# First norm of a hybrid decoder step: shift and scale in 256, 256 and 512 features, and a new order around them

## The chip, the cores and the metric

The kernel runs on one core of a Trainium2 chip. A core has a matrix engine (TensorE, PE), a vector engine (VectorE, DVE), a scalar engine (ScalarE, ACT), a general engine (GpSimd, POOL) and a queue engine that issues transfers (SyncE, SP); 16 DMA engines move data between HBM and the on-chip memory. The metric is device time in microseconds (us), the median of several runs. The kernel before takes 1035.17 us (three runs, 1034.39 to 1036.36).

## What is computed

One layer of a decoder trunk for 512 prompt tokens and 8 sample tokens (520 columns), model width 1024. What matters here is its beginning:

```python
def rms_norm(x, g):
    xf = x.astype(jnp.float32)
    y = xf * lax.rsqrt(jnp.mean(xf * xf, axis=-1, keepdims=True) + EPS)
    return (y * g.astype(jnp.float32)).astype(x.dtype)

def ada_modulation(c, ada_w, ada_b):
    m = (jax.nn.silu(c) @ ada_w + ada_b)[:, None, :]
    return jnp.split(m, 6, axis=-1)
...
    sh1, sc1, g1, sh2, sc2, g2 = ada_modulation(c, ada_w, ada_b)
    h = rms_norm(x, norm1_g) * (1.0 + sc1) + sh1
    z = h @ w_in
    cuts = list(np.cumsum([D_RNN, D_RNN, ATTN_W, ATTN_W, ATTN_W, N_HEADS, D_MODEL]))
    xr, gr, q, k, v, fl, ga, gb = jnp.split(z, cuts, axis=-1)
```

Behind it come a gated recurrence, attention over the prompt and over paged caches, the merge of both branches and a gated feed-forward part. All of it is float32, and each product of two float32 matrices is made of three products of parts.

## The kernel before

**Layout.** Activations stand transposed: a tile has 128 features on the partitions and 520 tokens as columns, so the width of 1024 is eight tiles, called features 0 to 7 below. Columns are worked on in two halves of 260 (`HALVES`); the last 8 columns are the sample tokens. Every operand of a product is split in a high part (a cast to the matmul type, `hi`, on ScalarE) and a low part (the rest, `lo`, on VectorE); one product is three matmuls, hi x hi, lo x hi and hi x lo (L527).

**The start, in program order.**
1. SP loads the parameters, the constants, the eight tiles of `x`, and the page table twice (`ptb`, `idx`, L424 and L426).
2. ScalarE squares `x` (L536), VectorE adds up (L538), TensorE sums over the partitions (`ss`, L543).
3. `first_mod` (L470) computes shift and scale of the first norm for half of the features, 512 at a time: for each of eight k it loads a block of `ada_w` (`araw`, 512 KB) and issues four matmuls, one for each group of 32 columns of the array (L476), 256 columns wide. `first_mod_end` (L480) copies the sum (`adas`), transposes it twice (`adaft`), adds the bias to get `mod` (L489) and forms the amplitude `n1amp` (L493).
4. The square root (L548) and the reciprocal (L549) give the reciprocal norm `r1`, and eight multiplications give `xn` (L552).
5. `first_h` (L496) makes the operand of a feature: ScalarE's `hh` (L499) for 512 prompt columns, GpSimd's two small operations for the 8 sample columns (L500, L501), ScalarE's cast of these (L503), VectorE's copy of the modulated tile (L502) and the low part `hl` (L504).
6. `q_weights` (L507) loads and splits the weights of two column tiles of q for four features: `wraw`, `whi` (L517), `wlo` (L518).
7. The products for the first six tiles of q run in two halves of the features. The first half (features 0 to 3) runs over two groups of three tiles, `g3` = 0 and 3, each with six PSUM banks, in an order k, tile, half of the columns. In the first group a k of the second `first_mod` (features 4 to 7) is placed behind every third product; in the second group, behind k = 0, stands its `first_mod_end` and `first_h` for features 4 to 7. The partial sums are copied out (L575). Then the weights of the second half are loaded and split, and a scheduler of products (`begin`, `product`) takes over, which adds the second half's sums (`qp`, L902).

**What sets the order.** The tile framework puts each engine's instructions in an order of its own from the program and its estimate of times; `tc.issue_after` holds instructions back behind a named one. Engines work through their own list in order. Buffers come from pools: seven for `araw` and cache pages (`pgp`), two for `wraw`, three each for `whi` and `wlo`, eight PSUM banks. An instruction that writes a buffer waits for the last reader of what was in it. GpSimd's gather of past forget values (`past_load`, L431) uses a `wraw` buffer. SP's transfers share eight semaphores, so each waits for the landing of the eighth before it.

Of the kernel before, what the change touches and what calls it, by code (L numbers as in the profile page):

```python
# [8 lines left out]
F32 = mybir.dt.float32  # L9
# [9 lines left out]
NP = 512  # L19
NS = 8  # L20
NT = NP + NS
H = 16
# [42 lines left out]
def kernel(ctx, tc, xT, par, gates, b_f, cst, cse, own, cache_k, cache_v, cache_lf, pt,  # L65
# [358 lines left out]
    sp.dma_start(ptb, pt.rearrange("a b -> (a b)")[None, :])  # L424
    idx = keep.tile([NS * NPAGE, 1], I32, name="idx")
    sp.dma_start(idx, pt.rearrange("a (b c) -> (a b) c", c=1))  # L426
# [43 lines left out]
    def first_mod(fh, acc, kqs):  # L470
        for kq in kqs:
            raw = pgp.tile([128, 2, 512], F32, name="araw", tag="pg")
            sp.dma_start(raw, ada_w[kq * 128:kq * 128 + 128, :2048].rearrange("p (v c) -> p v c", v=2)
                         [:, :, 512 * fh:512 * fh + 512])
# [5 lines left out]
    def first_mod_end(fh, acc):  # L480
        sb = slot("adas", 256)
        act.copy(sb, acc[:, :256])
        tp = bank(f"adaft{fh}")
        for b in range(2):
            pe.transpose(tp[:, b * 128:b * 128 + 128], sb[:, b * 128:b * 128 + 128], ident)
        tv = tp[:, :256].rearrange("p (b g c) -> p b g c", b=2, g=4)
        fs = slice(4 * fh, 4 * fh + 4)
        for v in (1, 0):
            dve.tensor_tensor(  # L489
                mod[:, v, fs].rearrange("p (q b) c -> p b q c", b=2), tv[:, :, 2 * v:2 * v + 2, 0:9],  # L490
                prm[:, fs, P_AB + v:P_AB + v + 1].rearrange("p (q b) c -> p b q c", b=2).to_broadcast([128, 2, 2, 9]),
                ALU.add)
        dve.scalar_tensor_tensor(amp1[:, fs], mod[:, 1, fs], 1.0, prm[:, fs, P_N1:P_N1 + 1].to_broadcast([128, 4, 9]),  # L493
                                 ALU.add, ALU.mult)
# [13 lines left out]

    def q_weights(fh, raw, ko, i):
# [5 lines left out]
        for k in range(0, 4, 2 if (fh, i) == (0, 0) else 4):  # L515
            ks = slice(k, k + 2 if (fh, i) == (0, 0) else 4)
            state["act"] = act.copy(hi[:, ks], src[:, ks])  # L517
            state["last"] = dve.tensor_tensor(lo[:, ks], src[:, ks], hi[:, ks].bitcast(F32), ALU.subtract)  # L518
# [25 lines left out]
    acc = [bank(f"adaf{fh}") for fh in range(2)]  # L544
    first_mod(0, acc[0], range(KT))
    r1 = slot("r1")
    for j, (t0, t1) in enumerate(HALVES):
        act.activation(r1[:, t0:t1], ssq[j][:, :HALF], AF.Sqrt, bias=eps, scale=1.0 / D)  # L548
        dve.reciprocal(r1[:, t0:t1], r1[:, t0:t1])  # L549
    for f in range(KT):  # L550
        t = slot("xn")
        dve.tensor_tensor(t, x[f], r1, ALU.mult)  # L552
        xn.append(t)
    raw = wraw()
    q_weights(0, raw, 0, 0)
    first_mod_end(0, acc[0])
    for f in range(4):
        first_h(f)
    q_weights(0, raw, 4, 2)
    raw = wraw()  # L560
    q_weights(0, raw, 0, 4)
    for g3 in (0, 3):
        banks = [bank(f"qp{i}_{j}") for i in range(g3, g3 + 3) for j in range(2)]
        for k in range(4):
            for n in range(6):
                q_matmuls(0, g3 + n // 2, n % 2, k, banks[n])
                if g3 == 0 and n % 3 == 2:
                    first_mod(1, acc[1], (2 * k + n // 3,))
            if g3 and k == 0:
                first_mod_end(1, acc[1])  # L570
                for f in range(4, KT):
                    first_h(f)
        for n in range(6):
            t0, t1 = HALVES[n % 2]
            act.copy(qpart[g3 + n // 2][:, t0:t1], banks[n][:, :HALF])  # L575
        if g3 == 0:
            flr = slot("flr", KT * H).rearrange("p (k c) -> p k c", k=KT)
# [1148 lines left out]
```

## Time and profile before

| | |
|---|---|
| median of three runs | 1035.17 us (1034.39 to 1036.36) |
| the profiled execution | 1036.26 us, span 1034.6 us |
| TensorE busy in 0 to 10, 10 to 20, 20 to 30 us | 0.38, 8.70, 7.11 us |
| TensorE busy in 30 to 60 us | 30.0 of 30 us |
| TensorE busy in 200 to 1034.6 us | 809.7 of 834.6 us |
| first product of q | 25.18 us after the span's start |
| first product of the second half of the features | 50.70 us |
| DMA moved | 207 MB, mean 200 GB/s |

Each profile is of one execution; times in it count from the span's start. Busy time of TensorE includes the tail of each matmul, which overlaps the next one, so what one matmul costs is read from the distance between starts. "Idle before, releaser" in brackets names the wait of that engine ahead of the row and what ended it.

### The profile page before, as it was taken

The page shows a single profiled execution, that of the slowest core. Times are in us where ns is not written, and L with a number is a line of the kernel's source. Part 1 is how long each engine was busy: PE and PEld are TensorE (multiplying, and loading weights), DVE is VectorE, ACT ScalarE, POOL GpSimd, SP SyncE. Part 2 cuts the span into 40 slices and gives each one's busy share as a digit, 9 for nine tenths or more (in the row PEclk, how much of TensorE's full clock was granted, in tenths as well). Part 3 has the DMA queues.
Part 4 walks back from the last instruction along what each step waited for, and adds up shares of the span by engine and source line. Part 5 has one row for each costly group of instructions (what it writes and reads, how often), then busy time and mean ns, then how long its engine had stood idle before and what let it go on. Part 6 is the DMA issues. An engine that isn't in the chain of part 4 may idle for free.

```text
span 1034.6 us, 21301 instructions
## 1 busy us (share of the span) xinstructions
PE 993.8 (96%) x7994; PEld 920.1 (89%) x7994; DVE 795.3 (77%) x1416; ACT 549.4 (53%) x1128; POOL 333.9 (32%) x431
## 2 busy tenths in 40 slices
PE   4999999999999999999999999999999999999994
PEld 2888989999898988878888989999999999999993
DVE  5547999988989977886665555878888888888763
ACT  4523675856682267776794234554444444445451
POOL 0224511112133235544430001494343342444022
PEclk9999999999999999999999999999999999999997
DMA  9898987787888999988675783324334234133222
GB/s 332 294 295 290 301 286 213 259 250 275 257 238 309 324 310 300 300 252 269 202 267 198 254 286 104 82 63 123 90 95 123 74 112 123 42 103 103 64 70 74
DMA packets 165419, 206.99 MB, mean 200 GB/s; under 512 B 9906, under 2 KB 126146, under 8 KB 165250
## 3 DMA queue, kind: packets, MB, share of 16 engines
q1 hardware_dynamic: 148594, 152.52, 47.7%
q0 software_dynamic: 13040, 46.67, 13.7%
q10 hardware_dynamic: 3680, 6.42, 1.7%
q8 instruction: 63, 1.03, 0.4%
q14 instruction: 42, 0.34, 0.1%
HBM read 192.49 MB, written 13.09 MB: 199 GB/s over the span
## 4 chain that ended last, share of the span: by engine, by line
PE 70%; DVE 12%; DMA 6%; ACT 4%; issue 4%; POOL 2%; SPq 1%; POOLq 0%; ACTq 0%; DVEq 0%
PE fo L305 9%; PE pb L305 4%; PE gb L305 4%; PE xr L305 3%; PE ga L305 3%; PE k L305 3%; PE wo L305 3%; PE v L305 3%; DVE wlo L250 2%; PE gr L305 2%; PE qp L527 2%; DVE pg L730 2%; PE pv L815 2%; PE po L1258 2%; PE ada L368 1%
## 5 line engine op out<-in xcount | busy, mean ns | idle before, releaser
L248 ACT CAST whi<-wraw 128x1024 fp32r<-128x1024 f32 (+1 forms) x79 | 82.0, 1039 | 117.9 <-PE pb L305 35.0
L250 DVE TENSOR_TENSOR wlo<-wraw,whi 128x1024 fp32r<-128x1024 f32 (+1 forms) x79 | 101.3, 1284 | 30.1 <-ACT whi L248 25.9
L305 PE MATMUL fo<-ach,wb 128*128 128x260 f32 x512 | 93.3, 282 | 0.0
L272 ACT CAST wb<-ws 128x512 fp32r<-128x512 f32 x72 | 44.8, 622 | 91.2 <-PE fo L305 63.6
L682 POOL DMA_DIRECT2D pg<-in_cache_k_dram x74 | 39.6, 535 | 142.4 <-DVE S L731 70.3
L305 PEld LDWEIGHTS fo<-ach,wb 128*128 128x128 f32 x512 | 78.8, 188 | 0.0
L273 DVE TENSOR_TENSOR wb<-ws,wb 128x512 fp32r<-128x512 f32 x72 | 67.5, 937 | 14.6 <-ACT wb L272 12.6
L273 DVE TENSOR_TENSOR wb<-wraw,wb 128x512 fp32r<-128x512 f32 x86 | 74.2, 863 | 5.1 <-ACT wb L272 4.4
L263 POOL TENSOR_TENSOR ws<-wraw 128x512 f32<-128x512 f32 x18 | 26.6, 1478 | 154.0 <-DMA wraw<-in_w_fi_dram 76.7
L305 PE MATMUL fo<-acl,wb 128*128 128x260 f32 x256 | 72.3, 282 | 0.0
L272 ACT CAST wb<-wraw 128x512 fp32r<-128x512 f32 x86 | 53.6, 623 | 33.6 <-ACT cp L1612 5.8
L730 DVE TENSOR_TENSOR pg<-pg,qb 128x1024 f32<-128x1024 f32 x48 | 58.0, 1227 | 2.5 <-DMA pg<-in_cache_k_dram 2.5
L731 DVE TENSOR_REDUCE S<-pg 128x16 f32<-128x1024 f32 x48 | 57.0, 1207 | 0.1
L1215 POOL TENSOR_SCALAR p<-p,mu 128x128 f32<-128x128 f32 (+3 forms) x28 | 35.9, 1294 | 49.9 <-DVE mu L1211 33.1
L397 POOL TENSOR_TENSOR ss<-ss,sq 128x260 f32<-128x260 f32 x18 | 13.8, 769 | 110.3 <-PE ada L368 58.9
L305 PEld LDWEIGHTS fo<-acl,wb 128*128 128x128 f32 x256 | 48.1, 188 | 0.0
L1209 ACT ACTIVATE p<-p,mu 128x128 f32<-128x128 f32 (+3 forms) x64 | 35.3, 553 | 15.9 <-DVE mu L1208 12.4
L305 PE MATMUL v<-hh,whi 128*128 128x260 f32 x128 | 37.3, 291 | 1.3 <-DVE pl L1229 1.3
L305 PE MATMUL ga<-hh,wlo 128*128 128x260 f32 x128 | 36.9, 288 | 0.9 <-DVE wlo L250 0.9
L305 PE MATMUL pb<-oh,whi 128*128 128x260 f32 x128 | 36.7, 287 | 1.0 <-ACT oh L1316 1.0
L305 PE MATMUL k<-hh,whi 128*128 128x260 f32 x128 | 37.3, 291 | 0.0
L305 PE MATMUL ga<-hh,whi 128*128 128x260 f32 x128 | 37.0, 289 | 0.0
(1092 smaller groups left out, 3990.7 us busy)
## 6 DMA issues: line engine op xcount, KB each, us to landing
araw<-in_ada_w_dram SPq DMA_DIRECT2D x48, 512.0 KB, 6.8
wraw<-in_w_fi_dram SPq DMA_DIRECT2D x44, 512.0 KB, 4.7
pg<-in_cache_k_dram POOLq DMA_DIRECT2D x42, 512.0 KB, 5.5
pg<-in_cache_v_dram SPq DMA_DIRECT2D x42, 512.0 KB, 5.8
wraw<-in_w_in_dram SPq DMA_DIRECT2D x34, 512.0 KB, 8.1
wraw<-in_w_in_dram SPq DMA_DIRECT2D x11, 1024.0 KB, 9.8
pg<-in_cache_v_dram POOLq DMA_DIRECT2D x22, 512.0 KB, 6.3
pg<-in_cache_k_dram POOLq DMA_DIRECT2D x32, 256.0 KB, 6.0
```

The lines of the kernel that those rows point to most:

```text
L248: state["act"] = act.copy(hi[:, :k1 - k0], src)
L250: state["last"] = dve.tensor_tensor(lo[:, :k1 - k0], src, hi[:, :k1 - k0].bitcast(F32), ALU.subtract)
L263: pool.tensor_tensor(s1, a21, a22, ALU.add)
L272: state["act"] = act.copy(t[:, :4], src)
L273: state["last"] = dve.tensor_tensor(t[:, 4:], src, t[:, :4].bitcast(F32), ALU.subtract)
L305: state["mm"] = pe.matmul(out[:, :HALF], lhsT=wt[k], rhs=at, start=k == 0 and m == 0, stop=k == nk - 1 and m == 2)
L527: state["mm"] = pe.matmul(b[:, :HALF], lhsT=wt, rhs=at[:, t0:t1], start=k == 0 and m == 0, stop=k == 3 and m == 2)
L682: done.append(eng.dma_start(pg, cache[bass.ds(r, 1), :, c0:c1].rearrange("a p c -> (a p) c")))
L730: dve.tensor_tensor(pg, pg, q, ALU.mult)
L731: last = dve.tensor_reduce(S[r // 2][:, c:c + H], pg.rearrange("p (h d) -> p h d", d=DH), AX.X, ALU.add)
L1209: act.activation(p[:, :n + 128], p[:, :n + 128], AF.Exp, bias=mu[:, 0:1], scale=-1.0, accum_out=mu[:, 1:2])
L1215: (pool.tensor_scalar(p, p, mu[:, 2:3], None, ALU.mult) if a and i + 1 < KT else act.activation(p, p, AF.Copy, scale=mu[:, 2:3]))
```

## The change

The modulation of the first norm comes in three parts instead of two: features 0 and 1 (256 columns), features 2 and 3 (256), features 4 to 7 (512). For the first two parts, blocks of 256 KB (`qraw`, rows of 1 KB) are loaded two to a buffer, and each matmul has 128 columns (`quarter_load`, `quarter_mod`). The first part stands ahead of the products, the second among the products of features 0 and 1, the third among those of features 2 and 3 of the first group and of features 0 and 1 of the second.

The reciprocals stand first on VectorE. For features 0 and 1, `xn`, `hh` and `hl` are made by halves of the columns (`early_norm`, `early_h`), and `xn` is modulated in place; the other `xn` follow. The weights of the first half of q are loaded for three column tiles and two features at a time (`q_load`, 384 KB) and split in `q_high` and `q_low`. The products of the first half go in groups (`q_group`) in an order half of the columns, feature, tile, not feature, tile, half. The loads of `ptb` and `idx` move behind these loads.

Cut to its core; `q_weights` and the copies are only rearranged:

```diff
-    sp.dma_start(ptb, pt.rearrange("a b -> (a b)")[None, :])
     idx = keep.tile([NS * NPAGE, 1], I32, name="idx")
-    sp.dma_start(idx, pt.rearrange("a (b c) -> (a b) c", c=1))
...
+    def quarter_load(q, kq):
+        if kq % 2 == 0:
+            quarters[q, kq // 2] = pgp.tile([128, 2, 2, 256], F32, name="qraw", tag="pg")
+        sp.dma_start(quarters[q, kq // 2][:, kq % 2],
+                     ada_w[kq * 128:kq * 128 + 128, :2048].rearrange("p (v c) -> p v c", v=2)
+                     [:, :, 256 * q:256 * q + 256])
+
+    def quarter_mod(q, acc, kqs):
+        for kq in kqs:
+            raw = quarters[q, kq // 2][:, kq % 2]
+            for g in range(4):
+                pe.matmul(acc[32 * g:32 * g + 32, :128], lhsT=silc[:, kq],
+                          rhs=raw[:, g // 2, 128 * (g % 2):128 * (g % 2) + 128],
+                          start=kq == 0, stop=kq == KT - 1, tile_position=(0, 32 * g))
...
+    def early_norm(j):
+        t0, t1 = HALVES[j]
+        for f in range(2):
+            state["last"] = dve.tensor_tensor(xn[f][:, t0:t1], x[f][:, t0:t1], r1[:, t0:t1], ALU.mult)
+
+    def early_h(j):
+        t0, t1 = HALVES[j]
+        e_ = min(t1, NP)
+        for f in range(2):
+            if j == 0:
+                h.append((slot("hh", dt=F32R), slot("hl", dt=F32R)))
+            t, (hi, lo) = xn[f], h[f]
+            a_, b_ = amp1[:, f, 0:1], mod[:, 0, f, 0:1]
+            first = act.activation(hi[:, t0:e_], t[:, t0:e_], AF.Identity, scale=a_, bias=b_)
+            if j:
+                pool.tensor_tensor(t[:, NP:], t[:, NP:], amp1[:, f, 1:9], ALU.mult)
+                pool.tensor_tensor(t[:, NP:], t[:, NP:], mod[:, 0, f, 1:9], ALU.add)
+                act.copy(hi[:, NP:], t[:, NP:])
+            dve.tensor_scalar(t[:, t0:e_], t[:, t0:e_], a_, b_, ALU.mult, ALU.add)
+            dve.tensor_tensor(lo[:, t0:t1], t[:, t0:t1], hi[:, t0:t1].bitcast(F32), ALU.subtract)
+        return first
...
-    first_mod(0, acc[0], range(KT))
+    raw = wp.tile([128, 4, 384], F32, name="wraw", tag="wraw", bufs=2)
+    for kq in range(6):
+        quarter_load(0, kq)
+    q_load(raw, 0, 0)
+    for kq in range(6, KT):
+        quarter_load(0, kq)
+    quarter_mod(0, accs[0], range(KT))
+    for kq in range(KT):
+        quarter_load(1, kq)
...
-        dve.reciprocal(r1[:, t0:t1], r1[:, t0:t1])
-    for f in range(KT):
-        t = slot("xn")
-        dve.tensor_tensor(t, x[f], r1, ALU.mult)
-        xn.append(t)
-    raw = wraw()
-    q_weights(0, raw, 0, 0)
-    first_mod_end(0, acc[0])
-    for f in range(4):
+        state["last"] = dve.reciprocal(r1[:, t0:t1], r1[:, t0:t1])
+    early_norm(0)
+    his = q_high(raw, 0, 0, 1)
+    with tc.issue_after(state["last"].ins):
+        q_low(*his, 0)
+    with tc.issue_after(first_mod_end(0, 1, accs[0]).ins):
+        first = early_h(0)
+        q_low(*his, 1)
+        early_norm(1)
+        with tc.issue_after(first.ins):
+            early_h(1)
+    for f in range(2, KT):
+        dve.tensor_tensor(xn[f], x[f], r1, ALU.mult)
+    q_load(raw, 2, 0)
+    q_split(raw, 2, 0)
+    sp.dma_start(ptb, pt.rearrange("a b -> (a b)")[None, :])
+    sp.dma_start(idx, pt.rearrange("a (b c) -> (a b) c", c=1))
...
+    q_group(0, 0, 0)
+    q_group(0, 0, 1, (0, 1), quarter)
+    q_group(0, 1, 0, (2, 3, 4), quarter)
+    q_group(0, 1, 1, (5, 6, 7), quarter)
+    first_mod_end(2, 1, accs[1])
+    first_h(2)
+    first_h(3)
+    acc = bank("adaf2")
+    q_group(0, 0, 2, (0,), half)
...
+    q_group(0, 1, 2, (1,), half)
+    q_group(0, 0, 3, (2,), half)
+    q_group(0, 1, 3, (3, 4), half)
...
+    q_group(3, 0, 0, (5,), half)
+    q_group(3, 1, 0, (6,), half)
+    q_group(3, 0, 1, (7,), half)
+    first_mod_end(4, 2, acc)
...
+    for f in range(4, KT):
         first_h(f)
...
+    for j, k in ((1, 1), (0, 2), (1, 2), (0, 3), (1, 3)):
+        q_group(3, j, k)
```

In `q_group(i0, j, k, kqs, mod)` the products of three tiles from `i0` with feature `k` are issued for half `j` of the columns, and then the modulation of the given `kqs`.

104 lines of the change are left out of this document (64 added, 40 removed).

## The prediction

> **What bounds the kernel now.** I read the page's busy shares first, then the start in stretches of ten microseconds (columns: busy time and count of TensorE, its weight loads, VectorE, ScalarE and GpSimd, then TensorE's clock, DMA share, GB/s).
>
> ```profile
> span 1034.6 us, 21301 instructions
> PE 993.8 (96%) x7994; PEld 920.1 (89%) x7994; DVE 795.3 (77%) x1416; ACT 549.4 (53%) x1128; POOL 333.9 (32%) x431
> ```
>
> ```profile
> 0.00:10.00 10.00, 0.38 (x1) 0.38 (x2) 2.10 (x3) 5.29 (x8) 0.56 (x7) 1.00 0.78 264
> 10.00:20.00 10.00, 8.70 (x56) 3.86 (x55) 7.83 (x9) 3.57 (x6) 0.00 (x0) 1.00 1.04 385
> 20.00:30.00 10.00, 7.11 (x45) 4.69 (x46) 8.71 (x17) 6.74 (x13) 4.81 (x8) 0.66 1.07 370
> ```
>
> TensorE idles 40.8 us in all, 13.8 of them in the first 30 us (9.6 + 1.3 + 2.9); in the other 1004.6 us it idles 27. So TensorE sets the time, and a change at the start is worth what it does to the moment at which TensorE has finished the same work. The chain of waits (start, duration, step) says what holds it there.
>
> ```profile
> 16.04 7.11 DMA wraw<-in_w_in_dram
> 23.15 0.02 issue
> 23.18 1.14 ACT whi L517 x2
> 24.31 0.82 ACT hh L499
> ...
> 25.18 3.85 PE qp L527 x15
> ...
> 33.39 1.28 PE qp L527 x9
> 34.67 0.57 PE adaf L476 x8
> ...
> 44.36 6.50 PE qp L527 x54
> ```
>
> The reader is to see three things. The first q product waits until 25.18 for transfers and then for a cast and the first `hh`. From there TensorE works without a gap. A q matmul takes 6.50 / 54 = 0.120 us. One k of the modulation (four matmuls over 256 columns, eight records) takes 0.57, and a round of nine products and one such k takes 1.85, so each switch between the two kinds costs 1.85 - 0.57 - 9 x 0.120 = 0.20 more. The first half of q (features 0 to 511) ends at 44.36 + 6.50 = 50.9. That moment is my yardstick: what does the change make of it, and of the products right behind it?
>
> **Part 1, the first product comes earlier.** Before it, VectorE now does two reciprocals, two half-width `xn`, one low part of 384 columns and the three small operations on `mod`, in place of two reciprocals, eight full `xn` and those three. Its rows (start, duration, operation), and ScalarE's:
>
> ```profile
> 14.24 3.42 DVE L549 RECIPROCAL r<-r 128x260 f32<-128x260 f32 x2 [1.84 <-ACT r L548]
> 17.69 4.97 DVE L552 TENSOR_TENSOR xn<-x,r 128x520 f32<-128x520 f32 x8
> ...
> 23.85 0.30 DVE L489 TENSOR_TENSOR mod<-adaft,prm 128x36 f32<-128x36 f32 x2 [1.19 <-PE adaft L485]
> 24.08 0.20 DVE L493 SCALAR_TENSOR_TENSOR n1amp<-mod,prm 128x36 f32<-128x36 f32 x1
> ...
> 50.56 0.70 DVE L504 TENSOR_TENSOR hl<-hr,hh 128x520 fp32r<-128x520 f32 x1
> 51.18 1.22 DVE L518 TENSOR_TENSOR wlo<-wraw,whi 128x1024 fp32r<-128x1024 f32 x1
> 52.34 0.43 DVE L902 TENSOR_TENSOR qp<-q,qp 128x260 f32<-128x260 f32 x1
> ```
>
> ```profile
> 14.60 0.48 ACT L548 ACTIVATE r<-ss,eps 128x260 f32<-128x260 f32 x1 [0.39 <-PE ss L543]
> ...
> 42.95 1.05 ACT L517 CAST whi<-wraw 128x1024 fp32r<-128x1024 f32 x1
> ...
> 46.51 0.20 ACT L503 CAST hh<-hr 128x8 fp32r<-128x8 f32 x1 [0.83 <-POOL hr L501]
> 46.61 0.82 ACT L499 ACTIVATE hh<-xn,mod,n1amp 128x512 fp32r<-128x512 f32 x1
> ```
>
> The reciprocals end at 17.66 in both kernels, because nothing ahead of them changes. Two `xn` of 260 columns (0.43 alone, about 0.35 back to back) reach 18.4; the low part of 384 columns, between 0.43 and 0.70, reaches 18.9; `mod` twice and `n1amp` (24.28 - 23.85 = 0.43) reach 19.3; the half-width `hh` (0.48, as the square root of that width) 19.8. First product at 19.9.
>
> The other branch is the transfers (TensorE's rows):
>
> ```profile
> 21.70 0.95 PE L476 MATMUL adaf<-araw,silc 128*32 128x256 f32 x8 [0.73 <-DMA araw<-in_ada_w_dram]
> 23.13 0.69 PE L485 MATMUL adaft<-cs,adas 128*128 128x128 f32 x2 [0.47 <-ACT adas L482]
> ```
>
> Now 8 x 512 KB = 4.19 MB have landed at 21.70. The changed kernel needs 8 x 256 KB and one weight block of 384 KB, 2.49 MB, so 1.70 MB less. At the 383 GB/s of the stretches below that is 4.4 us: 17.3. Its rows are 1 KB instead of 2 KB; where 1 KB weight rows land the stretch shows 351 GB/s, which adds 0.65: 17.9. Modulation, copy and transpose, half as wide, take about 1.1 where 21.70 to 23.85 is 2.15 now: `mod` could begin at 19.0. Both branches meet, and I keep 19.9, a gain of 5.3; bounds 19.7 and 21.0. The eight or so added transfer issues on SP, and the two page-table loads moved behind them, are covered: issues run ahead of landings, and the gather that needs the page table starts at 54.72 (row in part 4). GpSimd's register reads of that table now stand between the small additions for features 1 and 2, which part 3 puts some 5 us apart.
>
> **Part 2, work that comes back behind the start.** Before, half of the modulation lay in front of the first product; now only a quarter does, and the second quarter stands among the products. That is eight k of 128 columns. No row has that width. A k of 512 columns takes
>
> ```profile
> 85.48 0.99 PE ada L368 x8
> ```
>
> so 0.57 at 256 and 0.99 at 512 give 0.36 at 128 on a straight line; the upper bound is 0.57, if the eight weight loads and not the columns set it. I take 0.36: 2.9 in all. They stand in four places, four switches of 0.20; one more transpose is 0.1. Sum +3.8; bounds 3.0 and 5.5. VectorE's and ScalarE's halved instructions for features 0 and 1 (six more on VectorE) lie beside these products; if that cover failed they would cost about half a microsecond.
>
> **Part 3, a wait for features 2 and 3.** The first 36 products use features 0 and 1 alone. What follows the last k of the second quarter is: copy, transpose, `mod` twice, `n1amp`, together about 1.2, then `hh` of 512 columns 0.8, 2.0 in all. TensorE has, meanwhile, the transpose, one modulation k and one product, 0.8. So it idles +1.2; bounds 0 (other engines ahead) and 2.0.
>
> **Part 4, a wait at the second half.** In the order in which the changed program is built, ScalarE's third weight cast for the second half stands ahead of `hh` of features 6 and 7, and it needs the buffer that the very last product of the first half reads. GpSimd's gather of the past forget values, which needs that cast's low part, now stands ahead of the last small addition for feature 7; in the kernel before, it stands behind all of them:
>
> ```profile
> 48.23 0.57 POOL L501 TENSOR_TENSOR hr<-hr,mod 128x8 f32<-128x8 f32 x1
> 54.72 1.21 POOL L431 DMA_INDIRECT lfp<-in_cache_lf_dram,idx  x1 [5.93 <-DVE wlo L518]
> ```
>
> Count from the end E of the last product of the first half. Cast 1.05: E+1.1. `hh` of feature 6 0.82: E+1.9, and TensorE, which has 12 products of features 4 and 5 (1.45), waits 0.4. Low part 1.22 and `hl` 0.70: E+3.0, TensorE waits 0.6. Gather, 0.3 behind the low part as now: E+2.6 to E+3.9; addition 0.4 to 0.6, copy 0.2: E+4.6; TensorE, at E+3.5 by then, waits 1.1. Behind that copy stand the six copies that free the PSUM banks: 0.2 more. Sum +2.3; bounds 0 and 3.0.
>
> **Part 5, the clock.** Stretches of TensorE (busy time, clock, DMA share, GB/s):
>
> ```profile
> 18.53:21.94 3.41, 1.78 (x28) 0.99 1.06 372
> 21.94:25.35 3.41, 1.58 (x11) 0.50 1.09 351
> 25.35:28.76 3.41, 3.41 (x15) 0.51 1.05 386
> 11.70:15.10 3.40, 2.66 (x13) 1.00 1.03 383
> ```
>
> Now the products from 25.18 to 28.76 run at half clock, a loss of 1.8. The clock fell behind a stretch that was 52% busy and did not behind one that was 78% busy. In the changed kernel the stretch 18.53 to 21.94 would be about 60% busy (from 19.9 on). That is nearer to 52%, but where such a stretch lies in another execution no row says, so I count half of the loss as saved, -0.9; bounds 0 and -1.8. [...]
>
> **The sum.** -5.3 + 3.8 + 1.2 + 2.3 - 0.9 = +1.1 us. The profiled execution took 1036.26 (span 1034.6 and 1.66 around it), 1.1 above the median 1035.17 of the runs (1034.39 to 1036.36). From the first hundred microseconds on, both programs issue the same instructions in the same order, and TensorE has next to no slack there, so I let the shift stand and put it on the median: 1036.3.
>
> **Rivals.**
> - A, slower. The 128-column k cost 0.57 like the 256-column ones, at the same eight weight loads. Place: the second quarter among the first 36 products. Price 8 x 0.21 = 1.7, time 1038.0. For it: eight records start 0.07 us apart whatever waits. Against: 256 to 512 columns cost 0.42 more. It decides from 0.49 us for one k, where the sum passes +2.1.
> - B, faster. The waits of parts 3 and 4 do not show, because casts, gather and copies come before TensorE needs them: 1036.3 - 3.5 = 1032.8. For it: the kernel before has the same kinds of hand-over at 44 us without a gap. Against: the buffer and queue order just told.
> - C, the clock stays full through the start, for a reason that the 52% row does not cover: 1035.4. For it: work resumes 5 us earlier. Against: that row. [...]
> - D, the change does not do what it says: the 1 KB rows hold the first quarter back to the bound of 21.0, so the first product comes 4.2 earlier, not 5.3: 1037.4. Against: both branches reach 19.9 independently.
>
> **How the numbers follow.** About 0.2% (2.1 us) can be told from no change. The forecast, no measurable change at 1036.3, has 0.34; its own range is 1034.5 to 1038.0. A has 0.23, B 0.26, C 0.12, D 0.05. Faster is B, 0.26. Slower is A with 0.03 of D and the upper edge of the forecast, 0.03: 0.29. The rest, 0.45, is no change. All favourable bounds (-5.5 + 3.0 - 1.8) give 1030.9, all unfavourable (-4.2 + 5.5 + 2.0 + 3.0) 1041.5; a tenth of the chance left out on each side gives 1032.2 to 1039.2.
>
> **What would show each step.** Part 1: first `qp` matmul near 19.9, VectorE busy from the reciprocals to `n1amp`. Part 2: eight records of the small modulation in about 0.36 (0.57 speaks for A). Part 3: about 1.2 us of TensorE idle between the second transpose and the first product of feature 2, released by ScalarE's `hh`. Part 4: TensorE idle near 50 us, released by ScalarE's `hh` and VectorE's `hl` of features 6 and 7, and a GpSimd gather between two additions on 128 x 8. Part 5: clock around 0.5 for some 3 us or none. The prediction is wrong if the second half starts before 48 us, or if TensorE's idle time past 100 us differs by more than a microsecond.

## The result, and the profile after

The changed kernel is slower: a median of 1039.71 us over 22 runs (1035.26 to 1046.72) against 1036.52 us over 22 runs of the kernel before on the same chip (1032.19 to 1040.96), a ratio of 1.0036 [1.0022, 1.0050] (in brackets the 95% interval). Two later repeats gave 1.0035 [1.0018, 1.0053] (10 runs) and 1.0043 [1.0024, 1.0061] (12 runs). That is 3.6 to 4.5 us, where +1.1 was forecast. The profiled execution after took 1039.36 us (span 1037.7), the one before 1036.26 (span 1034.6).

One kernel's runs spread over 9 to 11 us and a profile shows one execution, so both kernels were profiled again: four executions before, five after. The table shows when certain products begin (us from the span's start). `qt` is the transpose of a finished tile of q, `ga` a merge gate, `pa` the projection of the recurrent branch, `po` the attention over the prompt and `fo` the last product of the feed-forward part. The rows are in order of time, so the last column says where the difference arose.

| first product of (unless the row says last) | before, 4 executions (mean) | after, 5 executions (mean) | difference of the means |
|---|---|---|---|
| q, first half (`qp`) | 25.18 to 25.98 (25.69) | 19.95 to 20.63 (20.27) | -5.4 |
| q, second half | 50.70 to 52.23 (51.62) | 48.37 to 51.41 (50.04) | -1.6 |
| `qt`, right behind the first tile of the second half | 56.46 to 57.98 (57.38) | 56.71 to 59.76 (58.65) | +1.3 |
| last `qt` | 100.33 to 101.39 (100.91) | 100.18 to 103.22 (102.22) | +1.3 |
| `ga` with the low part of its weights | 107.31 to 108.79 (107.94) | 108.05 to 111.85 (109.38) | +1.4 |
| `pa` | 305.76 to 307.70 (307.08) | 307.20 to 310.41 (309.05) | +2.0 |
| `po` | 384.83 to 390.62 (387.83) | 390.65 to 393.38 (391.75) | +3.9 |
| `fo` of `ach` with `whi`, last | 1003.36 to 1008.57 (1006.38) | 1009.94 to 1012.21 (1011.12) | +4.7 |

To `qt` the change behaves as forecast: 5.4 gained, given back to +1.3. Another 3.4 us comes between the last `qt` and the end, where the forecast had nothing.

The page after, its head, and the stretches of the start (columns as in the prediction):

```profile
span 1037.7 us, 21458 instructions
PE 997.5 (96%) x8058; PEld 924.9 (89%) x8058; DVE 798.6 (77%) x1426; ACT 549.2 (53%) x1132; POOL 335.1 (32%) x431
```

```profile
0.00:10.00 10.00, 0.22 (x1) 0.23 (x2) 2.10 (x3) 5.37 (x8) 0.56 (x7) 1.00 0.77 262
10.00:20.00 10.00, 7.76 (x73) 4.76 (x73) 7.59 (x13) 5.26 (x10) 0.00 (x0) 1.00 1.09 356
20.00:30.00 10.00, 9.52 (x105) 7.66 (x109) 7.83 (x17) 3.34 (x9) 1.15 (x4) 0.83 1.07 370
17.00:20.40 3.40, 1.57 (x23) 0.76 (x20) 3.05 (x10) 1.46 (x4) 0.11 (x1) 1.00 1.10 348
20.40:23.80 3.40, 3.40 (x22) 2.73 (x21) 3.37 (x10) 1.44 (x5) 1.04 (x4) 0.50 1.09 353
51.20:54.60 3.40, 1.77 (x11) 1.15 (x9) 2.29 (x3) 1.71 (x5) 1.58 (x2) 0.99 1.01 341
54.60:58.00 3.40, 3.37 (x15) 3.37 (x16) 1.47 (x3) 1.64 (x6) 0.19 (x1) 0.51 1.09 413
```

TensorE's idle time in the first 30 us is 9.8 + 2.2 + 0.5 = 12.5 us (13.8 before), yet its clock halves twice, from 20.40 and from 54.60, each time behind a stretch in which it was about half busy (1.57 and 1.77 of 3.40).

The chain of waits of the kernel after, at the start (start, duration, step):

```profile
11.47 6.32 DMA qraw<-in_ada_w_dram
...
17.84 0.47 PE adaf L481 x8
...
19.01 0.26 DVE mod L505 x2
19.27 0.14 DVE n1amp L511
...
19.44 0.61 ACT hh L528
...
20.09 1.44 PE qp L588 x6
21.53 0.99 PE adaf L481 x10
...
26.40 0.79 PE adaf L481 x24
27.19 1.28 PE qp L588 x9
28.47 0.84 PE adaf L481 x24
```

The first `qp` starts at 20.09, as forecast, behind `mod`, `n1amp` and a half-width `hh`. Twenty-four records are three small k: 0.79 and 0.84 for three, 0.27 for one. The chain into the second half of q, in the same kernel:

```profile
50.13 1.06 ACT whi L578
...
51.21 1.24 DVE wlo L579
52.45 0.29 issue
52.74 1.37 POOL lfp L429
...
54.14 0.23 POOL hr L542
...
54.38 0.20 ACT hh L544
...
54.63 5.09 PE q L588 x28
```

It is the queue order of part 4, step by step: weight cast, low part, gather of past forget values, and only then the last small addition and its copy, which TensorE awaits. TensorE's rows of the two hand-overs (operation, start, duration, and in brackets its wait and what ended it):

```profile
29.65 0.33 PE L499 MATMUL adaft<-cs,adas 128*128 128x128 f32 x1 [0.39 <-ACT adas L496]
...
31.31 0.39 PE L588 MATMUL qp<-hh,whi 128*128 128x260 f32 x1 [0.44 <-ACT hh L540]
...
51.95 0.39 PE L588 MATMUL q<-hh,whi 128*128 128x260 f32 x1 [0.46 <-ACT hh L540]
...
53.10 0.39 PE L588 MATMUL q<-hl,whi 128*128 128x260 f32 x1 [0.41 <-DVE hl L545]
...
54.63 0.58 PE L588 MATMUL q<-hh,whi 128*128 128x260 f32 x1 [0.80 <-ACT hh L544]
```

The three waits of the second half add up to 1.67 us. What they cost is read from the distance between its first product and the first `qt`: 5.75 or 5.76 in all four executions before, 8.34 or 8.35 in four of the five after (+2.6), and 9.67 in the one above, whose products from 54.60 ran at half clock. The recorded waits are less than the cost for two reasons. A matmul's record is 0.28 long while the next starts 0.12 later, so 0.16 of each gap counts as busy. And the first product behind a wait has a record of 0.39, and the next one starts 0.23 behind it instead of 0.12 (both read at full clock).

Past 110 us, one row of stretches of each kernel, before and then after:

```profile
110.00:1034.60 924.60, 898.84 (x7248) 844.36 (x7246) 731.85 (x1302) 505.16 (x1039) 302.86 (x365) 0.99 0.61 187
```

```profile
110.00:1037.70 927.70, 902.19 (x7262) 847.34 (x7261) 736.20 (x1305) 505.99 (x1043) 304.62 (x366) 0.99 0.60 187
```

TensorE idles 25.8 us before and 25.5 after. Over all nine executions the means are 25.5 and 25.8. So the later loss is hardly idle time: it lies in TensorE's busy time, in products at half clock and products that start further apart.

### The profile page after: what moved, and what is told of

It is laid out like the page before. It is cut to its first block, busy times and chain, and to the rows that moved or that the text cites. A ratio compares the mean times of both kernels' runs of the same rounds, so it can differ in the third digit from the quotient of the medians.

```text
span 1037.7 us, 21458 instructions
## 1 busy us (share of the span) xinstructions
PE 997.5 (96%) x8058; PEld 924.9 (89%) x8058; DVE 798.6 (77%) x1426; ACT 549.2 (53%) x1132; POOL 335.1 (32%) x431
## 4 chain that ended last, share of the span: by engine, by line
PE 68%; DVE 11%; issue 6%; DMA 5%; ACT 5%; POOL 3%; POOLq 1%; SPq 0%; DVEq 0%; ACTq 0%
PE fo L305 9%; PE pb L305 4%; PE gb L305 4%; PE k L305 4%; PE wo L305 3%; PE ga L305 3%; PE v L305 3%; PE gr L305 2%; DMA wraw<-in_w_in_dram 2%; PE xr L305 2%; PE qp L588 2%; PE pv L915 2%; DVE wlo L250 2%; PE po L1358 2%; PE q L588 1%
## 5 line engine op out<-in xcount | busy, mean ns | idle before, releaser
L250 DVE TENSOR_TENSOR wlo<-wraw,whi 128x1024 fp32r<-128x1024 f32 (+1 forms) x79 | 99.0, 1254 | 33.0 <-ACT whi L248 30.9
L273 DVE TENSOR_TENSOR wb<-wraw,wb 128x512 fp32r<-128x512 f32 x86 | 76.9, 894 | 4.8 <-ACT wb L272 4.3
L273 DVE TENSOR_TENSOR wb<-ws,wb 128x512 fp32r<-128x512 f32 x72 | 65.0, 902 | 13.8 <-ACT wb L272 12.4
L263 POOL TENSOR_TENSOR ws<-wraw 128x512 f32<-128x512 f32 x18 | 23.9, 1325 | 156.2 <-DMA wraw<-in_w_fi_dram 120.4
L397 POOL TENSOR_TENSOR ss<-ss,sq 128x260 f32<-128x260 f32 x18 | 13.8, 766 | 109.3 <-PE ada L368 59.1
L305 PE MATMUL gb<-hh,whi 128*128 128x260 f32 x128 | 37.2, 290 | 0.0
```

What stands on the lines that cost most here:

```text
L250: state["last"] = dve.tensor_tensor(lo[:, :k1 - k0], src, hi[:, :k1 - k0].bitcast(F32), ALU.subtract)
L263: pool.tensor_tensor(s1, a21, a22, ALU.add)
L273: state["last"] = dve.tensor_tensor(t[:, 4:], src, t[:, :4].bitcast(F32), ALU.subtract)
L305: state["mm"] = pe.matmul(out[:, :HALF], lhsT=wt[k], rhs=at, start=k == 0 and m == 0, stop=k == nk - 1 and m == 2)
```

## The experiments

The theories were these. First: the waits at the second half of q, and the half clock behind them, are the loss; without them the kernel gets faster than the one before. Rival: what is gained early does not arrive, because a meeting point further on (the weights of `ga`, near 107 us) sets the time. Later: everything behind the start runs in another order, or the difference lies in the clock that an execution happens to get. Ratios are to the kernel before in the same set of runs.

**The gather held back.** In `first_h` and at `past_load`, on the kernel after:

```diff
-        pool.tensor_tensor(t[:, NP:], t[:, NP:], mod[:, 0, f, 1:9], ALU.add)
+        state["h_pool"] = pool.tensor_tensor(t[:, NP:], t[:, NP:], mod[:, 0, f, 1:9], ALU.add)
...
-            past_load()
+            with tc.issue_after(state["h_pool"].ins):
+                past_load()
```

> GpSimd's gather of the past logits is issued behind all small additions instead of ahead of feature 7's. Theory (the loss is the waits at the second half plus the half-clock stretch they bring on): of the gather's 1.37 us on GpSimd only its last part is on the path, because feature 7's first addition would otherwise wait for feature 7's share of the queue alone. The third wait (0.80 us, ended by the 128x8 cast of feature 7) shrinks to about 0.2, the waits in 51.2 to 54.6 fall from 1.67 to about 1.0 us, that stretch is then about 70% busy; the clock is in doubt there: first qt transpose at about 59.0 with the half rate kept, 57.5 without it (changed kernel: 59.56). Rival (each wait costs only itself, the clock has nothing to do with it): 59.56 - 0.6 = 59.0, with the half-rate stretch still there. Time 1037.5 to 1039.

Measured: 1040.43 us, 1.0039 [1.0025, 1.0053]. The second half went from its first product to `qt` in 7.33 us: 1.0 of the 2.6 was the gather's. The gain was gone at `ga`:

```profile
112.38 0.58 PE L305 MATMUL ga<-hh,wlo 128*128 128x260 f32 x1 [3.75 <-DVE wlo L250]
```

**The weight cast held back**, behind the last `hh` and `hl`:

```diff
-    q_weights(1, raw, 0, 4)
+    with tc.issue_after(state["h_act"].ins), tc.issue_after(state["h_dve"].ins):
+        q_weights(1, raw, 0, 4)
```

> ScalarE's third cast of weights is issued behind the casts and activations of features 4 to 7; the gather then also comes behind the small additions. Theory: all three waits at 51.9 to 54.6 go (2.1 us by the starts of the products around them), TensorE is busy from the first product of the second half on, so no stretch of half clock at 54.6 to 58.0 (1.6 us): first qt transpose at 59.56 - 3.7 = about 55.9, time about 3.7 us under the changed kernel's, 0.5 us under the kernel before. The third cast then ends near 54 instead of 51.2, and its weights are wanted at the third tile of q (about 56), so it is not late. Rival (the waits cost only themselves and the rest of the 3.2 us is the extra modulation work): qt at 59.56 - 2.1 = about 57.5 and 1 us above the kernel before. Second rival (the cast is then itself late): a wait of TensorE for wlo of the later tiles, 0.5 to 1 us at about 55 to 57.

Measured: 1044.25 us, 1.0074 [1.0049, 1.0099], slower than without the edit. The second half took 6.29, so 2.05 of its 2.6 came back, as the buffer and queue order says. The loss is elsewhere; VectorE's and TensorE's rows of this kernel near `ga`:

```profile
109.93 1.35 DVE L827 TENSOR_TENSOR pg<-pg,qb 128x1024 f32<-128x1024 f32 x1 [3.57 <-DMA pg<-in_cache_k_dram]
...
113.89 1.21 DVE L250 TENSOR_TENSOR wlo<-wraw,whi 128x1024 fp32r<-128x1024 f32 x1
```

```profile
115.16 0.58 PE L305 MATMUL ga<-hh,wlo 128*128 128x260 f32 x1 [4.10 <-DVE wlo L250]
```

On VectorE a product on a cache page, which waits 3.57 us for the page to land, stands ahead of the low part of the `ga` weights, and the low part starts 3.96 behind it (113.89 against 109.93). The edit is at 50 us; the order that it disturbed is at 110.

**TensorE kept busy through the waits at 52 us** by 13 unused products of 252 columns (4, 3 and 6) behind the products of the first tile of the second half:

```diff
+        def fill(n):
+            with tc.issue_after(state["mm"].ins):
+                for _ in range(n):
+                    last = pe.matmul(bs[0][:, HALF:512], lhsT=qw[1, 0][0][0], rhs=h[4][0][:, :512 - HALF],
+                                     start=False, stop=False, skip_group_check=True)
+            return tc.issue_after(last.ins)
```

> Nothing is moved on ScalarE, VectorE and GpSimd; 13 products of 252 columns (0.11 us each) whose result is not used are put into the three waits of TensorE at the start of the second half, 4, 3 and 6. This keeps the waits (the operands come no earlier) and takes away only the idleness. Theory (idleness in 51.2 to 54.6 halves the clock of the next 3.4 us): granted clock stays at 1.00 in 54.6 to 58.0, the first qt transpose comes 1.2 to 1.6 us sooner than 59.56, at 58.0 to 58.4, the time falls by the same. Rival (the clock falls for another reason, or the half-rate stretch costs nothing since others are late too): qt at 59.6 or, with the added products in the way, up to 60.5, and the time the same or up to 1 us more than the changed kernel's.

Measured: 1040.01 us, 1.004 [1.0023, 1.0057]. The clock held there, and from its first product to `qt` the second half took 8.70, which is 0.36 more than the 8.34 without the fillers at full clock. That proves nothing for the fillers: without them it held too in four of five executions.

**TensorE kept busy ahead of the first product**, by three unused fp32 products:

```diff
+    for _ in range(3):
+        last = pe.matmul(banks[0, 0][:, HALF:512], lhsT=ident, rhs=x[0][:, :512 - HALF], start=True, stop=True)
+    with tc.issue_after(last.ins):
+        q_group(0, 0, 0)
```

> Three fp32 products of 252 columns (0.38 us each, as the sums of squares' products), result not used, are put between the transpose of the first modulation (18.64) and the first product (20.09), where TensorE idles 1.12 us. They raise the busy share of 17.0 to 20.4 from 1.57 to about 2.7 of 3.4 us. Theory: no half clock at 20.4 to 23.8; of the 1.7 us that this stretch loses, 0.7 to 1.7 come back (part may go to waits for the small casts and the differences of features 0 and 1, which the half rate hid): first product of the second half at 48.2 to 49.2 instead of 49.89, and the rest shifts with it, unless GpSimd and ScalarE are the ones that set the second half's wait; then it is lost there again. Rival (the first stretch's half rate is not brought on by the idle 1.12 us): clock 0.50 at 20.4 to 23.8 as before, 49.9 or up to 50.2.

Measured: 1037.85 us, 1.0012 [0.9991, 1.0033], level with the kernel before. Its interval overlaps that of the kernel after, so the gain from the edit isn't established. The profile shows the clock and the meeting point. First the stretches that answer to 17.00 and 20.40 above:

```profile
17.00:20.40 3.40, 2.91 (x31) 1.53 (x23) 2.83 (x9) 1.22 (x5) 0.00 (x0) 1.00 1.10 349
20.40:23.80 3.40, 3.40 (x35) 2.78 (x34) 3.37 (x10) 1.88 (x6) 1.15 (x4) 1.00 1.10 355
```

At full clock the second half begins at 48.84 and the last `qt` at 100.66, 2.36 earlier than in the profile of the kernel after. Then TensorE stands at `ga`; its rows, and those of SP (load issued) and ScalarE (cast) for the weights:

```profile
109.11 0.39 PE L305 MATMUL ga<-hh,whi 128*128 128x260 f32 x1 [2.42 <-ACT whi L248]
110.37 0.39 PE L305 MATMUL ga<-hh,wlo 128*128 128x260 f32 x1 [0.87 <-DVE wlo L250]
```

```profile
98.42 1.01 SPq L212 DMA_DIRECT2D wraw<-in_w_in_dram  x2
```

```profile
108.01 1.04 ACT L248 CAST whi<-wraw 128x1024 fp32r<-128x1024 f32 x1 [7.02 <-DMA wraw<-in_w_in_dram]
```

and the same two of the kernel after:

```profile
99.86 2.26 SPq L212 DMA_DIRECT2D wraw<-in_w_in_dram  x2
```

```profile
106.97 1.05 ACT L248 CAST whi<-wraw 128x1024 fp32r<-128x1024 f32 x1 [4.67 <-DMA wraw<-in_w_in_dram]
```

The load was issued 1.44 earlier and its cast came 1.04 later: 9.6 us from issue to cast instead of 7.1. In the profile after, GpSimd issued four loads of cache pages within these 7.1 us (at 100.09, 102.44, 103.85 and 105.31), and the DMA engines' mean busy share was 0.95, at 300 GB/s. So a gain of 2.36 us became a loss of 1.04 at this place (110.37 against 109.33), in this execution.

**A buffer of its own for the gather**, so that it does not wait for a `wraw` buffer. In exchange the heap of activations gave up four buffers:

```diff
-    heap = ctx.enter_context(tc.tile_pool(name="heap", bufs=60))
+    heap = ctx.enter_context(tc.tile_pool(name="heap", bufs=56))
...
-        t = wp.tile([NS * NPAGE, 2048], F32, name="lfp", tag="wraw", bufs=2)
+        t = keep.tile([NS * NPAGE, 2048], F32, name="lfp")
```

It was run alone on the kernel after, then with the held cast and gather, then with the three unused products as well, and alone on the kernel before:

> The gather of the past logits gets a buffer of its own (four heap buffers fewer pay for it) instead of one of the two that the weights' loads rotate through. It no longer waits for the difference of the weights, and the load of the first weights behind q (ga's) no longer waits for the difference of q's last tile (which ends near 98.6 in the changed kernel and is followed by the load's issue at 99.86, the weights' arrival at 106.97 and ga's first wlo product at 109.33). Theory (the second half's first tile loses time by the waits and the half clock, and about 107 us in, all kernels so far wait for the same load): the third wait shrinks as in e1, the first qt transpose comes at 58 to 59.6, ga's products wait for nothing, and the first wlo product of ga is at 107.5 to 109. Time 0 to 1.5 us under the changed kernel's. Rival (ga's wait is set by the cache pages on the DMA engines, not by the buffer): ga still waits 1 to 4 us.

> As l1_own, and besides the third cast of weights stands behind the activations of features 4 to 7 on ScalarE (as in e2_cast) and the gather behind the small additions on GpSimd. Theory: from the second half's first product to the first qt transpose 6.0 to 6.4 us (changed kernel 9.67, e2_cast 6.29, kernel before 5.76), and nothing is lost again at ga, so that the 3.4 us arrive at the end: 1035.5 to 1037 (up to 1.7 us of it by the length of the half-clock stretch at the start, 3.4 us or 6.8 us in the runs so far). Rival (the gain is always lost again further down, since the loads and not TensorE set the pace up to 110 us): qt as said, but ga's first wlo product at 109 or later, and the end at 1039 or above.

> As l2_cast, and the three products of unused result between the first modulation's transpose and the first product (as in s1_start). Theory: clock 1.00 from 17 us on, the first product of the second half at 48.8, the first qt at about 55.0, no wait at ga: 1.0 to 3.0 us under l2_cast and 1.0 to 2.0 us under the kernel before, 1033 to 1035. Rival (loads set the pace): as l2_cast, 1039 or above, with a longer wait at ga.

> The kernel before, with nothing but the gather's own buffer (and four heap buffers fewer). In the kernel before, ga's first wlo product waits 0.92 us for the difference of weights that arrive near 105.2. Theory: that wait goes, 0.5 to 0.9 us less, and a gap of 0.8 us at the gates stays. Rival (pages on the DMA engines set it, or the heap's four buffers are missed elsewhere): the same time or up to 1 us more.

Measured: 1053.33 us, 1.0181 [1.0149, 1.0213]; 1052.84, 1.0165 [1.0135, 1.0194]; 1051.08, 1.0152 [1.0125, 1.0179]; on the kernel before 1050.51, 1.0143 [1.0117, 1.0170]. All four missed. Against the profile after, the first of them loses about 8 us between 363 and 368 us, far from the gather, so these runs tell more of a smaller heap than of the gather. TensorE's rows of the first and of the last show what else the edit moved, a block of the later modulation and one of the first:

```profile
97.80 1.92 PE L368 MATMUL ada<-araw,silc 128*32 128x512 f32 x4 [3.45 <-DMA araw<-in_ada_w_dram]
```

```profile
20.83 1.08 PE L476 MATMUL adaf<-araw,silc 128*32 128x256 f32 x8 [3.49 <-DMA araw<-in_ada_w_dram]
```

On the kernel before, with the gather's load out early, the first modulation waits 3.49 for its weights and the first `qp` starts at 28.55, 3.4 later than without the edit.

**The kernel after again, the start's clock on the kernel before, and two combinations.** The kernel before got two unused products behind each of k = 5 and 6 of its first modulation (k counts from 0) and three ahead of the first `qp`. The combinations are the held cast with the three unused products on the kernel after, and the same with the order of the first cache pages changed:

```diff
-    KEYS = dict(zip(range(42), (2, 2, 1, 0, 2, 2, 2, 2,
+    KEYS = dict(zip(range(42), (1, 2, 1, 1, 2, 2, 2, 2,
```

> The changed kernel again, unedited, as a yardstick for the others of this set. Its first half-clock stretch lasted 3.4 us in one profile, while e1_gather and e2_cast, whose first 50 us are the same, showed 6.8 us (23.8 to 27.2 at 0.57 to 0.59) and reached the second half 1.45 us later. Theory: the length varies from execution to execution, so here the first product of the second half is at 49.9 or at 51.3, and the granted clock from 23.8 on says which; the first qt comes 9.7 us behind it if the waits are followed by a half-clock stretch, about 8.3 if not. Time 1038.5 to 1040.5. Rival (the length is a property of each kernel): 49.9 again.

> The kernel before with products of unused result in its idle stretches at the start: two fp32 products of 252 columns behind each of the last modulation's sixth and seventh part, three behind the transposes. Theory: its clock stays at 1.00 from 17 to 30 us, the second half starts at 50.70 - 1.8 = 48.9 or a little later, and the first wlo product of ga comes no earlier than 106.5 to 107.6, since it waits for the difference of weights whose load is issued behind other work: the wait of 0.92 grows to 1.5 to 2.7, and the end moves by 0 to -0.9 us. Rival (TensorE sets the pace everywhere): ga 1.8 us sooner, end 1.8 us sooner, 1033.3.

> e2_cast (third cast and gather behind the operands of features 4 to 7) and s1_start (products of unused result ahead of the first product) together. Theory: clock 1.00 throughout the first 60 us, second half at 48.2 to 48.8, first qt at 54.5 to 55.2, 4.4 to 5 us under the changed kernel's 59.56. What of it arrives at the end is set at ga's weights: e2_cast's first wlo product of ga was at 115.16, because VectorE's queue has a product on a cache page ahead of it that came late; 1038 to 1042. Rival (what is gained early arrives at the end): 1035.

> g1_cast_start with the first four numbers of key pages per product tile changed from 2, 2, 1, 0 to 1, 2, 1, 1: one pair of page loads fewer ahead of ga's weights, and one more behind them. Theory (the page loads and ga's weights share the DMA engines and VectorE's queue, and these set ga): the first wlo product of ga at 106 to 109 and the time 2 to 5 us under g1_cast_start's, 1034 to 1037, if the pages are not missed later on. Rival (the pages are not what holds ga's weights): ga as in g1_cast_start, the time the same or worse.

Measured: the kernel after 1040.81 us, with full clock through the start in its profile and the second half at 48.37; the kernel before with a full clock at its start (mean clock of its profile 0.993) 1041.79, 1.0053 [1.0036, 1.0069] (four runs); held cast and products 1042.92, 1.0055 [1.0037, 1.0073]; with the other page order 1040.50, 1.0043 [1.0024, 1.0062]. The page order mends the meeting point, as these TensorE rows of the last kernel show, with `ga` behind the tile before it and no wait:

```profile
107.29 0.28 PE L305 MATMUL ga<-hh,whi 128*128 128x260 f32 x1
107.41 0.28 PE L305 MATMUL ga<-hh,wlo 128*128 128x260 f32 x1
```

That is 1.9 us earlier than in the profile after, and the median stays where it was: in this execution half clock stood for 6.8 us from 385 and for 3.4 from 460. Against the kernel with the old page order `ga` came 6.8 us earlier and the median is 2.4 lower, with intervals that overlap. So the meeting point alone is not the cause. Where the expectations speak of q's last tile at the meeting point, the tile ahead of `ga` is the second of `xr`. The kernel before with its clock held began the second half at 50.37 and `ga` at 106.94, earlier than without the edit, and was slower all the same. Its engines and SP issue in the order of the kernel before from start to end, apart from the seven products (and one pair on VectorE at 184 us, which changes places between executions of the unedited kernel too). Yet its profile took 936.9 us from the last `qt` to the end, where the four executions before took 930.4 to 935.1 (mean 933.2) and the five after 934.7 to 938.8 (mean 936.7). So a loss like that of the change came without any new order. What makes it isn't explained.

**Three more executions of each kernel**, for the table above:

> The kernel before, unedited, for a second profile. If the start's half clock is a property of the kernel: clock about 0.5 from 22 to 28.7 us, 1.8 us lost, second half at 50.7, first wlo product of ga at 107.6 with a wait of 0.9. If it is the execution's: clock 1.00 at the start, second half up to 1.8 us sooner, and then a wait at ga that is longer by what was gained. At the first attention tile (ptt to po near 376 to 388): no loss if it is the change's, 1 to 2.5 us of half clock in some executions if not.

> The changed kernel, unedited, for a third profile. The waits in the second half's first tile (0.46, 0.41 and 0.80 us) are there whatever the clock does; the half-clock stretch behind them in about half of the executions. First wlo product of ga at 108.0 (no half clock) to 109.4.

> As r1_before. If the loss of the changed kernel is downstream of 110 us, the kernel before keeps its distance of about 0 to 1 us from its first profile at 300, 400 and 560 us; if downstream losses are the execution's, it too shows 1 to 3 us there.

> As r1_after; the four profiles of the changed kernel against the three of the kernel before: at ga +0.4 to +2.0 us, between ga and the end another 1 to 3 us, of which half-clock stretches are the scattered part.

> The kernel before, unedited, a fourth profile. If the loss behind 107 us is the change's: from the first pa product (near 307) to the first po product (near 388) 79 to 81 us. If it is the execution's: anything up to 84, as 83.3 in r1_before, with a half-clock stretch behind the wait near 386.

> The changed kernel, unedited, a fifth profile and five rounds. From the second half's first product to the first qt 8.3 us without a half-clock stretch, 9.7 with one (kernel before 5.76). From pa to po 81 to 84.5 us if the loss behind 107 us is the change's; 79 to 81 in this profile would speak for the execution. Ratio of the times 1.0035 as in the two earlier sets, within 0.0015.

The profiled spans were 1036.3, 1031.1 and 1034.5 before and 1038.4, 1040.0 and 1039.3 after. They show two things. Half-clock stretches (each 3.4, 6.8 or 10.2 us long; the last 10 to 13 us, in which TensorE has no products left, not counted) add up to 8.5 us in the mean of four executions before and to 8.9 in five after. They cost TensorE 3.6 and 4.4 us (busy time by one minus the clock, summed), so the clock has 0.8 of the 4.7 us between the profiles. And the delay of +1.3 at `qt` stands in the means, then grows by 0.1 to `ga`, 0.5 to `pa`, 2.0 to `po` and 0.8 to the end.

## Why the prediction was wrong, by its steps

The forecast of 1036.3 is 3.4 below the measured median. Of this, 1.35 is the base (1036.52 in the larger set, 1035.17 in the three runs that it stood on); the other 2.1 is the change itself (+3.2 between the medians, +1.1 forecast). The table's +4.7 is of four and five single executions and lies above what the runs show. The forecast was no measurable change; slower had a chance of 0.29, mostly for rival A, which did not happen.

- **Part 1, right.** First `qp` at 20.09, forecast 19.9. Both branches met: VectorE idled 0.35 until the transpose that `mod` needs was done. Rival D falls.
- **Part 2, right in kind, too large.** One small k took 0.27, forecast 0.36, in place of the 0.57 of rival A. The eight k stand in three places of the program, where the prediction counted four. The whole term was not measured alone: from the first `qp` to the second half parts 2, 3 and 5 gave +3.8 in the means, forecast +4.1. Rival A's time lay nearer to the result, for a reason that is not there.
- **Part 3, right in kind, 0.4 too large.** TensorE waits 0.44 for `hh`, and 0.39 for the copy ahead of the transpose, 0.83 in all; forecast 1.2.
- **Part 4, right.** The waits of 0.46, 0.41 and 0.80 stand in the forecast order with the forecast releasers, and cost 2.6, forecast 2.3. The held cast, which takes the cause away, gave 2.05 back. Rival B, that they do not show, falls.
- **Part 5, right in the mean, wrong as a property of the kernel.** Half clock in the first 60 us cost 2.7 us in the mean before (1.6 to 3.9) and 2.0 after (0 to 3.4), a gain of 0.7 where 0.9 was forecast. The spread of one kernel is larger than this gain. Rival C, a full clock through the start, came in one execution of five.
- **The sum to `qt`, right, with some luck.** Forecast -5.3 + 4.1 + 2.3 = +1.1; in the means -5.4 + 3.8 + 2.9 = +1.3 (the 2.9 has 0.3 of half clock in it). Two errors of opposite sign nearly cancel.
- **The step that failed** is the one behind the sum: "both programs issue the same instructions in the same order, and TensorE has next to no slack there, so I let the shift stand". What follows the last `qt` was put at nothing, and it measured +3.4 in the means. The first half of the sentence nearly holds. Lined up by names and shapes (buffer numbers left out), TensorE's 7315 matmuls from the last `qt` on come in the same order in all nine executions. On the other engines and in SP's transfers the order differs at some places up to 137 us, and behind that nowhere (but for the pair at 184 us). VectorE before, then after:

```profile
91.86 0.27 DVE L874 TENSOR_TENSOR cvp<-prm 128x24 f32<-128x24 f32 x2
...
92.99 1.22 DVE L726 TENSOR_TENSOR pg<-pg,qb 128x1024 f32<-128x1024 f32 x1
```

```profile
93.19 1.23 DVE L826 TENSOR_TENSOR pg<-pg,qb 128x1024 f32<-128x1024 f32 x1
...
94.44 0.23 DVE L974 TENSOR_TENSOR cvp<-prm 128x24 f32<-128x24 f32 x2
```

The page product stands behind these small `cvp` products before and ahead of them after. But only 0.4 of the 3.4 us has come by 142 us; the other 3.0 come where every engine has the same order in both kernels. So what failed is the conclusion: the same order and little idle time on TensorE did not keep the shift as it was.

Of these 3.4, in the means of the nine executions, 1.5 is half clock past 110 us (0.9 us lost before, 2.4 after), 0.2 is idle time, and the rest, 1.7, is products that start further apart. The first of the three is not established as a property of the change: it is two stretches in four executions before and seven in five after. Those near 282 us follow a wait of 1.8 us that is the same in both kernels (2.7 in one execution before, without half clock). Near 387 the waits differ from execution to execution (TensorE idles 0 to 1.9 us in 378 to 387.3 before, 0.6 to 1.7 after), and near 459 half clock came in one execution, after.

Of the rest, 0.9 arises between `pa` and `po`, and 0.5 can be seen alone, between the first and the last `fo` product. In this stretch TensorE has no wait and the full clock (before, after, and the kernel before with seven unused products):

```profile
712.94:1017.86 304.92, 304.92 (x2547) 304.86 (x2546) 245.93 (x473) 144.29 (x299) 107.25 (x80) 1.00 0.32 93
```

```profile
715.54:1020.94 305.40, 305.40 (x2548) 305.34 (x2547) 248.30 (x475) 145.62 (x304) 108.67 (x80) 1.00 0.32 92
```

```profile
714.48:1019.86 305.38, 305.38 (x2547) 305.32 (x2546) 246.31 (x473) 144.36 (x299) 107.94 (x80) 1.00 0.33 92
```

The same stretch took 304.92 or 304.93 in all four executions before and 305.39 or 305.40 in all five after, for the same products in the same order. So these 0.5 us belong to the program and not to the execution, and the third row shows that they need no new order. The held cast and the page order did move `ga`, to 115.16 and to 107.41, but in the means the change moves `ga` by only 0.1 more than the last `qt`. What makes products start further apart no run shows: this cause is open. The comparison of orders leaves out which buffer an operand lies in, and no run varied that.

The prediction's own test for this step, a difference of over a microsecond in TensorE's idle time past 100 us, did not fire in the means (26.3 before, 26.5 after). Between the two first profiles it is 26.7 against 25.7, less idle time in the slower kernel. It was the wrong test: a record of 0.28 us with starts 0.12 apart hides gaps up to 0.16, and a slower clock counts as busy (3.37 of 3.40 us at a clock of 0.51, from 54.60 in the profile after). The starts of named products, compared between the two kernels, would have fired. The range ended at 1039.2; its sum of all unfavourable bounds, 1041.5, held the result.

No version beat the kernel before.

## What to carry to other kernels

An early edit in a kernel whose order a scheduler makes is not finished where its own instructions end: compare the starts of the same named products all along both programs, in several executions of each, before believing that a shift stands. The same order of instructions is not enough: here 3.0 us came where no order differed. A wait that is removed is worth its length only up to the next place where all engines meet (here 2.36 us gained became 1.04 lost at `ga`, in one execution); look there first for what is late next. Do not judge a loss of a few tenths of a per cent by one profile of each kernel.

## What was not expected of the hardware

**The clock.** It halved behind short waits, for 3.4, 6.8 or 10.2 us, and in some executions only. TensorE's row of one wait and the stretch behind it, in the profile before and then in another execution of the same kernel:

```profile
280.63 0.50 PE L979 MATMUL gate<-xch,gws 128*128 128x260 f32 x2 [1.83 <-ACT gate L980]
```

```profile
280.63:284.03 3.40, 3.40 (x18) 3.40 (x19) 3.40 (x5) 3.09 (x9) 0.85 (x2) 0.60 0.92 316
```

```profile
281.70 0.50 PE L979 MATMUL gate<-xch,gws 128*128 128x260 f32 x2 [1.83 <-ACT gate L980]
```

```profile
281.70:285.10 3.40, 3.40 (x28) 3.40 (x29) 3.40 (x5) 3.08 (x9) 0.84 (x2) 1.00 0.94 319
```

The same wait of 1.83 us, the same instructions, and a mean clock of 0.60 with 18 matmuls in one, of 1.00 with 28 in the other. In the profile after it halved at 54.60 behind three waits of 1.67 us in all, and in the profile before at 21.94 behind waits of 0.18, 0.72 and 0.73 us (TensorE's rows at 18.97, 20.33 and 21.70). What decides whether it halves behind such a wait no run shows.

**The landing of weights.** The same load of `ga` weights took 7.1 us from issue to cast in the profile after and 9.6 in that of the three unused products, though it was issued earlier (98.42 against 99.86). In both, the cast waited for the landing (7.02 and 4.67 us) and came at 108.01 against 106.97: in these two executions an earlier issue did not bring an earlier landing.
